# One hybrid layer on one core: no gather rows from the 364th to the dense loop, the low part of the U tile behind the slot's rows, inputs loaded earlier, the last norms interleaved

## The chip, the cores and the metric

The kernel runs on one core of a Trainium2 chip. The time is the device time of one execution in microseconds; lower is better. Engines are named as the profile names them: PE (TensorE) multiplies matrices, DVE (VectorE) and ACT (ScalarE) work elementwise, POOL (GpSimd) issues indirect DMAs (gathers), SP (SyncE) issues most other DMAs. An engine runs its instructions in the order in which they stand, and so does SP's queue of DMA issues.

## What is computed

The reference is one layer on x of shape (1, 1024, 1024) in float32: a mixer (a gated linear recurrence and a state-space group, both behind one projection), added to x, then a retrieval feed-forward ("PEER"), added too, and a final RMS norm. The change lies in the second half:

```python
def block(xb):                       # 128 tokens at a time
    q = (xb @ wq).reshape(TOK_BLOCK, PEER_HEADS, PEER_QDIM)
    s1, s2 = q[..., :PEER_HALF] @ k1.T, q[..., PEER_HALF:] @ k2.T
    ...                              # top 16 of each, then top 16 of their sums: e, g
    u_sel = u_tab[e]                 # 8 heads x 16 experts of 16384
    act = gelu(einsum('thkd,td->thk', u_sel, xb))
    return einsum('thk,thkd->td', g * act, v_tab[e])
...
h = h + peer_ffn(rms_norm(h, norm2_g), ...)
return rms_norm(h, normf_g)
```

Each of the 1024 tokens picks 128 of 16384 experts; each expert is a row of `u_tab` and a row of `v_tab`.

## The kernel before

The 1024 tokens are 8 blocks of 128. Three blocks (NG = 3) are computed as the formula stands: for each of the 128 experts per token a row of U is gathered for all 128 tokens (one indirect DMA of 512 KB on POOL, L1263) and multiplied with the token's x and summed by one DVE instruction (`CUSTOM_DVE_ANT_0 row<-row,xg` in the profile, `ISA row,act<-row,xg` in the order of instructions). After 128 such U rows, Gelu and the gates, 128 V rows are gathered and accumulated into `hb` (`SCALAR_TENSOR_TENSOR hb<-row,act,hb`). One of these 256 steps of a block is called a row here: 3 x 256 = 768 rows in all. `mg.units` counts them; the pool `rows` holds eight (ROWS = 8), so that at most seven gathers are asked ahead. `xg` (x of the block) and `hb` (the residual) come by DMA, and `finish` norms a block and stores it.

The other five blocks (ND = 5) are computed densely, against all 16384 experts: `first` multiplies a tile of U (128 experts) with all 640 tokens and applies Gelu, a gate matrix G weighs the result, and `second` multiplies it with V and accumulates over all experts. Floats are split in a high and a low part (`uh`, `ul`; `vh`, `vl`; `hh`, `hl`; the high part by ACT, the low part by DVE), and each product is three matmuls.

This runs in two stages.

- *The early stage.* `ahead` computes `first` for 97 of the 128 tiles and stores the results in DRAM (A_d, L1412), loading U tiles (`ur`, L1318). `build` makes the gate matrix: top-k on DVE, one-hot tiles (`ohA`, `ohB`), matmuls (`gp`), copies into `gs` by ACT, and stores of 2 MB of `gs` into G_d (L1218). The rows run beside this. The order is set by a planner (`Merge`): every piece of work is a generator, engines have planned busy times, and the generator with the lowest planned time plus a bias goes next. What a generator yields it waits for: None, the name of a flag, or a function. After a function has come true, the generator's time is put to PE's planned time. Rows have a pace of at least 2 us; `gate` yields None in this stage.
- *The dense loop.* 32 turns `c` of four tiles each, in an order written out by hand. In a turn PE does `first` for one tile of the next turn (48 matmuls), then `second` for token blocks 0, 1, then 2, 3 and 4 tile by tile. `pair()` gives the PSUM for a block, with two buffers; `add` adds it to h (`h<-h,vp` on DVE). Between these pieces stand seven slots, `rows_of(0)` to `rows_of(6)`; each lets so many rows run as bring the spent share of the rows that are left up to its part of a turn. Here rows ignore the gate. `raw` has three buffers for the U and V loads (`ur` L1505, `vr` L1352); loads stand where an earlier user has just freed one.

`prologue` leads from one stage to the other: the first V tiles, G tiles (`gt`, L1454) and A_d tiles (`hr`, L1348). The pools of V lie where `gs` lay. `last` is the end of the final turn: `second` for blocks 2, 3, 4, each followed by the `finish` of the block before, with its own load of the norm's weights `nf` (L1308) and its store (L1313).

Of the kernel before, what the change touches and what calls it, by code (L numbers as in the profile page):

```python
# [7 lines left out]
F32 = mybir.dt.float32  # L8
# [4 lines left out]
AF = mybir.ActivationFunctionType  # L13
# [5 lines left out]
P = 128  # L19
D = 1024  # L20
# [952 lines left out]
GT = 32  # L973
ROWS = 8
PACE = 2.0


def peer(tc, a, cst, pools, h, nx, mg):
# [25 lines left out]
    def split_to(hi, lo, src):  # L1004
        S.activation(hi, src, AF.Copy)
        V.tensor_tensor(lo, src, hi.bitcast(F32), ALU.subtract)
# [269 lines left out]
        return r  # L1276

    def gate():
        return (lambda: mg.units < share[0]) if share else None

    def gather(n):

        xg = gp.tile([P, D], F32, name="xg", tag="xg", bufs=1)
        nc.sync.dma_start(xg, X_d[n])
        act = gp.tile([P, P], F32, name="act", tag="act", bufs=1)
        for k in range(P):
            ub = take()
            yield gate()
            V.tensor_tensor_reduce(ub, ub, xg, 1.0, 0.0, ALU.mult, ALU.add, act[:, k:k + 1])
            mg.units += 1  # L1290
        hb = gp.tile([P, D], F32, name="hb", tag="hb", bufs=1)
        nc.sync.dma_start(hb, H_d[n])
        S.activation(act, act, AF.Gelu_apprx_tanh)
        yield
        V.tensor_tensor(act, act, gw[n], ALU.mult)
        yield
        for k in range(P):
            vb = take()
            yield gate()
            V.scalar_tensor_tensor(hb, vb, act[:, k:k + 1], hb, ALU.mult, ALU.add)  # L1300
            mg.units += 1
        finish(ND + n, hb)
        yield

    def finish(b, x):
        sq = rows.tile([P, D], F32, name="sqf", tag="row")
        nf = rows.tile([P, D], F32, name="nf", tag="row")
        nc.sync.dma_start(nf, a["gf"].partition_broadcast(P))  # L1308
        st = gp.tile([P, 3], F32, name="st", tag="st")
        S.activation(sq, x, AF.Square, accum_out=st[:, 0:1])  # L1310
        rsqrt_cols(mg, st[:, 1:2], st[:, 2:3], st[:, 0:1], 1.0 / D)
        V.scalar_tensor_tensor(x, x, st[:, 2:3], nf, ALU.mult, ALU.mult)
        nc.sync.dma_start(out_v[:, b], x)  # L1313
# [159 lines left out]
    def rows_of(slot):  # L1473

        spread[0] += SLOTS[slot] / sum(SLOTS) * left / (nch - 0.6)
        while mg.units < 2 * NG * P and left - (2 * NG * P - mg.units) + 1 <= spread[0]:
            row()

    def second(p_, b, t, first, last):
        bs = slice(b * P, b * P + P)  # L1480
        for i in range(2):
# [25 lines left out]
    def split_u(c):  # L1507
        uh = pu.tile([P, 8, P], F32R, tag="uh", name="uh")
        ul = pu.tile([P, 8, P], F32R, tag="ul", name="ul")
        split_to(uh, ul, raw_u.pop(c))  # L1510
        return uh, ul

    def prologue():
        now = [tile(0, n) for n in range(JC)]
# [49 lines left out]
    def dense():  # L1564
        now = [tile(0, n) for n in range(JC)]
        u = nextu.pop()
        carry = None
        for c in range(nch):
            more = c + 1 < nch
            nx = [tile(c + 1, n) for n in range(JC)]  # L1570

            now[3].high()
            fs = ()
            if more:
                nx[2].hr = phh.tile([P, TD], F32, name="ha", tag="ha", bufs=1)
# [12 lines left out]

            pr = [pair()]
            for jj, t in enumerate(now):  # L1590
                second(pr[0], 0, t, jj == 0, jj == JC - 1)
            if c + 2 < nch:
                u = split_u(c + 2)
            load_v(c + 1, 2)
            rows_of(1)

            if more:
                nx[0].turn()
            pr.append(pair())
            for jj, t in enumerate(now):  # L1600
                second(pr[1], 1, t, jj == 0, jj == JC - 1)
            add(0, pr[0])
            if not more:
                finish(0, acc[0])
            rows_of(2)
            if not more:
                last(now, pr)
                return

            pr.append(pair())  # L1610
            for jj, t in enumerate(now):
                second(pr[2], 2, t, jj == 0, jj == JC - 1)
                if jj == 0:
                    second(total, 4, t, c == 0, False)
                    add(1, pr[1])
                    nx[0].weigh()
                    rows_of(3)
                    pr.append(pair())
                second(pr[3], 3, t, jj == 0, jj == JC - 1)
                if jj:  # L1620
                    second(total, 4, t, False, False)
                if jj:
                    nx[jj].weigh()
                    nx[jj - 1].low_h()
                    if jj == 1:
                        load_h(c + 2, 0)
                    elif jj == 2:
                        load_h(c + 2, 1)
                    rows_of(3 + jj)
                    if jj == 3:  # L1630
                        weights(c + 2) if c + 2 < nch else None
                        add(2, pr[2])
                    nx[jj - 1].low_v()
                    if jj == 1:
                        load_v(c + 1, 3)
                    elif jj == 2:
                        load_u(c + 3)
                    else:
                        load_v(c + 2, 0)
                if jj < 3:  # L1640
                    nx[jj + 1].turn()
                    nx[jj].high()
            carry = 3, pr[3]
            now = nx

    def last(now, pr):

        for b in (2, 3, 4):
            p_ = pair() if b < 4 else total
            for jj, t in enumerate(now):  # L1650
                second(p_, b, t, b < 4 and jj == 0, jj == JC - 1)
            if b == 2:
                add(1, pr[1])
                finish(1, acc[1])
            else:
                add(b - 1, p0)
                finish(b - 1, acc[b - 1])
            p0 = p_
        add(4, total)
        finish(4, acc[4])  # L1660

    with tc.manual_schedule():
        dense()
# [81 lines left out]
```

## Time and profile before

| | us |
|---|---|
| median of 3 runs | 2668.85 (2663.75 to 2673.37) |
| profiled execution, its own time | 2657.8 |
| its span from first to last instruction | 2656.0 |
| PE busy | 2508.6 (94%) |
| DVE busy | 2363.7 (89%) |
| ACT busy | 1322.6 (50%) |
| POOL busy | 1157.8 (44%) |
| start of the first `second` matmul of the dense loop (chain of waits) | 1541.0 |

Times in the views are from the span's start. A row of a timeline has start, duration, engine, line, operation, output<-inputs and, in brackets, how long the engine was idle before it and what ended that. Most lines are L146, a helper that records every operation, so work is told apart by its tiles. SPq and POOLq are DMA issues; their duration is the time that the issue held the queue. A wait for several things is put down to the one that came last.

### The profile page before, as it was taken

Reading aid. Unit: us, or ns where it says so; the run is one execution under the profiler, and the core shown is the slowest. Engines: PE = TensorE matmul, PEld = TensorE weight load, DVE = VectorE, ACT = ScalarE, POOL = GpSimd, SP = SyncE. Lnnn points to the kernel's source line nnn. Section 1 sums busy time; section 2 is a strip of 40 time slices with the busy share of each in tenths; the row PEclk is TensorE's granted clock in tenths of the full one; section 3 lists DMA queues with packets and bytes.
Section 4 is the critical chain, followed back from the end, with each engine's and each line's share of the span. In section 5 each row is a group of like instructions: output and inputs, shape, how many; then the busy total and the mean of one; then the engine's idle time right before and its main releaser. Section 6 shows DMA issues by size and latency. Waiting matters only on the chain.

```text
span 2656.0 us, 40788 instructions
## 1 busy us (share of the span) xinstructions
PE 2508.6 (94%) x14623; PEld 2272.5 (86%) x14623; DVE 2363.7 (89%) x4549; ACT 1322.6 (50%) x2404; POOL 1157.8 (44%) x777
## 2 busy tenths in 40 slices
PE   7998999998999999999999699999899999999996
PEld 6776889998999999998999688888788888888885
DVE  7898559998999999999999589999888888999996
ACT  5566334332774956838749443344444343333333
POOL 0000000353754847748547345554445545555440
PEclk9999999999999999999999899999999999999998
DMA  5113124687999999999989989999899999999994
GB/s 176 34 44 108 59 88 136 227 280 273 326 382 317 366 378 309 393 330 365 398 277 388 373 316 333 328 330 329 306 327 323 329 326 327 329 329 331 331 325 131
DMA packets 302971, 755.40 MB, mean 284 GB/s; under 512 B 28976, under 2 KB 127472, under 8 KB 298032
## 3 DMA queue, kind: packets, MB, share of 16 engines
q0 software_dynamic: 110592, 402.70, 42.1%
q1 hardware_dynamic: 186480, 339.95, 36.1%
q10 hardware_dynamic: 5696, 10.15, 1.1%
q8 instruction: 115, 1.88, 0.3%
q14 instruction: 88, 0.72, 0.1%
HBM read 665.54 MB, written 85.98 MB: 283 GB/s over the span
## 4 chain that ended last, share of the span: by engine, by line
PE 59%; DVE 23%; DMA 9%; ACT 5%; issue 3%; SPq 0%; ACTq 0%; DVEq 0%
PE vp L146 25%; PE ap L146 16%; PE total L146 6%; DMA A_d<-aa 4%; PE qp L146 3%; PE gp L146 3%; ACT ohB L146 3%; PE wop L146 3%; DVE oh L146 2%; DVE row L146 2%; DVE ul L146 2%; DMA ur<-in_uT_dram 1%; DVE hb L146 1%; DVE ix L146 1%; DVE ci L146 1%
## 5 line engine op out<-in xcount | busy, mean ns | idle before, releaser
L1263 POOL DMA_INDIRECT row<-in_peer_u_dram,idx x384 | 560.9, 1461 | 942.9 <-DVE scv L146 473.7
L1263 POOL DMA_INDIRECT row<-in_peer_v_dram,idx x384 | 594.2, 1547 | 456.9 <-DVE hb L146 332.3
L146 PE MATMUL ap<-xDl,uh 128*128 128x320 f32 x2048 | 654.4, 320 | 26.0 <-ACT aa L146 25.3
L146 PE MATMUL ap<-xDh,ul 128*128 128x320 f32 x2048 | 646.9, 316 | 9.0 <-DVE ul L146 8.9
L146 PE MATMUL ap<-xDh,uh 128*128 128x320 f32 x2048 | 644.8, 315 | 0.0
L146 DVE SCALAR_TENSOR_TENSOR hb<-row,act,hb 128x1024 f32<-128x1024 f32 x384 | 491.7, 1280 | 4.4
L146 DVE CUSTOM_DVE_ANT_0 row<-row,xg 128x1024 f32<-128x1024 f32 x384 | 458.5, 1219 | 12.8 <-DMA xg<-X_d 7.3
L146 PEld LDWEIGHTS ap<-xDl,uh 128*128 128x128 f32 x2048 | 391.8, 191 | 30.1 <-ACT aa L146 27.8
L146 PE MATMUL vp<-vl,hh 128*128 128x512 f32 x1024 | 400.5, 391 | 11.6 <-DVE vl L146 9.8
L146 PEld LDWEIGHTS ap<-xDh,ul 128*128 128x128 f32 x2048 | 391.5, 191 | 12.1 <-DVE ul L146 10.7
L146 PE MATMUL vp<-vh,hl 128*128 128x512 f32 x1024 | 399.6, 390 | 0.0
L146 PE MATMUL vp<-vh,hh 128*128 128x512 f32 x1024 | 399.5, 390 | 0.0
L146 PEld LDWEIGHTS ap<-xDh,uh 128*128 128x128 f32 x2048 | 391.0, 191 | 0.0
L146 ACT ACTIVATE gq<-gt 128x640 f32<-128x640 f32 x128 | 175.3, 1369 | 328.8 <-DVE hr L146 324.4
L146 DVE TENSOR_TENSOR ul<-ur,uh 128x1024 fp32r<-128x1024 f32 x128 | 155.8, 1218 | 92.5 <-ACT uh L146 92.5
L146 PEld LDWEIGHTS vp<-vl,hh 128*128 128x128 f32 x1024 | 193.0, 188 | 52.4 <-DVE vl L146 10.7
L146 PEld LDWEIGHTS vp<-vh,hh 128*128 128x128 f32 x1024 | 192.9, 188 | 40.3
L146 PEld LDWEIGHTS vp<-vh,hl 128*128 128x128 f32 x1024 | 193.0, 189 | 38.8
L146 PE MATMUL gp<-ohB,ohA 128*128 128x128 f32 x1280 | 198.1, 281 | 24.5 <-ACT gs L146 16.9
L146 ACT ACTIVATE aa<-ap 128x320 f32<-128x320 f32 x194 | 84.8, 438 | 244.0 <-PE ap L146 194.7
L146 ACT ACTIVATE ohB<-ohB,kt 128x128 f32<-128x128 f32 x480 | 205.1, 502 | 0.0
L146 PEld LDWEIGHTS gp<-ohB,ohA 128*128 128x128 f32 x1280 | 179.4, 193 | 30.0 <-ACT gs L146 18.0
(442 smaller groups left out, 4488.3 us busy)
## 6 DMA issues: line engine op xcount, KB each, us to landing
ur<-in_uT_dram SPq DMA_DIRECT2D x128, 512.0 KB, 6.5
vr<-in_peer_v_dram SPq DMA_DIRECT2D x128, 512.0 KB, 6.2
gt<-G_d SPq DMA_DIRECT2D x32, 1280.0 KB, 9.4
G_d<-gs SPq DMA_DIRECT2D x19, 2048.0 KB, 25.6
A_d<-aa SPq DMA_DIRECT2D x96, 320.0 KB, 8.6
hr<-A_d SPq DMA_DIRECT2D x96, 320.0 KB, 5.8
wqr<-in_wq_dram SPq DMA_DIRECT2D x31, 512.0 KB, 3.9
row<-in_peer_u_dram,idx POOLq DMA_INDIRECT x384, 7.4
```

Of the source, the lines that this page charges most:

```text
L146: return fn(*args, **kw)
L1263: G.indirect_dma_start(out=r, out_offset=None, in_=a["peer_v" if at >= P else "peer_u"], in_offset=bass.IndirectOffsetOnAxis(ap=idx[n][:, ...
```

## The change

Four edits, in the order of the diff.

1. `gate` now yields a function in the early stage too: a row goes on while fewer than EARLY = 363 are done. So from the 364th on no row runs until the dense loop, which takes all that are left. As the gate is a function, every early row also has its planned time put to PE's.
2. `xg` of the next block is loaded right after the last U row of a block instead of at the next block's start, and `hb` after the 65th U row instead of after the last.
3. `split_u` is cut in two: ACT's `uh` stays where it was, DVE's `ul` comes behind `rows_of(1)`.
4. `last` loads `nf` once, and the norms of blocks 0 to 4 are generators whose steps stand between the matmul groups; block 4 is finished in two halves of 512 columns.

```diff
+EARLY = 363
...
     def gate():
-        return (lambda: mg.units < share[0]) if share else None
+        return lambda: mg.units < (share[0] if share else EARLY)
+
+    held = []
+    def fetch_xg(n):
         xg = gp.tile([P, D], F32, name="xg", tag="xg", bufs=1)
         nc.sync.dma_start(xg, X_d[n])
+        return xg
+
+    def gather(n):
+        xg = fetch_xg(n) if n == 0 else held.pop()
         act = gp.tile([P, P], F32, name="act", tag="act", bufs=1)
         for k in range(P):
             ub = take()
             yield gate()
             V.tensor_tensor_reduce(ub, ub, xg, 1.0, 0.0, ALU.mult, ALU.add, act[:, k:k + 1])
             mg.units += 1
-        hb = gp.tile([P, D], F32, name="hb", tag="hb", bufs=1)
-        nc.sync.dma_start(hb, H_d[n])
+            if k == P // 2:
+                hb = gp.tile([P, D], F32, name="hb", tag="hb", bufs=1)
+                nc.sync.dma_start(hb, H_d[n])
+        if n + 1 < NG:
+            held.append(fetch_xg(n + 1))
...
     def split_u(c):
         uh = pu.tile([P, 8, P], F32R, tag="uh", name="uh")
         ul = pu.tile([P, 8, P], F32R, tag="ul", name="ul")
-        split_to(uh, ul, raw_u.pop(c))
-        return uh, ul
+        r = raw_u.pop(c)
+        S.activation(uh, r, AF.Copy)
+        yield
+        V.tensor_tensor(ul, r, uh.bitcast(F32), ALU.subtract)
+        yield uh, ul
...
-            if c + 2 < nch:
-                u = split_u(c + 2)
+            su = split_u(c + 2) if c + 2 < nch else None
+            if su:
+                next(su)
             load_v(c + 1, 2)
             rows_of(1)
+            if su:
+                u = next(su)
...
     def last(now, pr):
+        nf = rows.tile([P, D], F32, name="nf", tag="row")
+        nc.sync.dma_start(nf, a["gf"].partition_broadcast(P))
+
+        def norm(b):
...
+            if b < 4:
+                S.activation(sq, x, AF.Square, accum_out=st[:, 2:3])
+                yield
+            else:
+                for i in range(2):
+                    xi = x[:, 512 * i:512 * i + 512]
+                    V.tensor_tensor(xi, xi, total[:, i], ALU.add)
+                    V.tensor_tensor_reduce(sq[:, 512 * i:512 * i + 512], xi, xi, 1.0, 0.0, ALU.mult, ALU.add,
+                                           st[:, i:i + 1])
+                    yield
+                V.tensor_tensor(st[:, 2:3], st[:, 0:1], st[:, 1:2], ALU.add)
...
+        for jj, t in enumerate(now):
+            second(total, 4, t, False, jj == JC - 1, (0,))
+        add(3, p0)
+        next(g[3])
+        for _ in g[2]:
+            pass
+        for jj, t in enumerate(now):
+            second(total, 4, t, False, jj == JC - 1, (1,))
```

How this moves instructions shows at three places. The first is DVE at the end of the early stage. Before, up to the first weighing of an A_d tile (`ul` belongs to U tiles of `ahead`, `vl` to V tiles of `prologue`; of the nine V rows that run in this stage the last four are shown):

```order
L146 TENSOR_TENSOR ul_16172<-ur_16169,uh_16171 128x1024
L146 SCALAR_TENSOR_TENSOR hb_16176<-row_16140,act_12642,hb_16176 128x1024
L146 SCALAR_TENSOR_TENSOR hb_16176<-row_16213,act_12642,hb_16176 128x1024
L146 SCALAR_TENSOR_TENSOR hb_16176<-row_16216,act_12642,hb_16176 128x1024
L146 SCALAR_TENSOR_TENSOR hb_16176<-row_16252,act_12642,hb_16176 128x1024
L146 TENSOR_TENSOR vl_16182<-vr_16107,vh_16180 128x1024
L146 TENSOR_TENSOR vl_16256<-vr_16210,vh_16254 128x1024
L146 TENSOR_TENSOR hr_16284<-hr_16284,gq_16292 128x640
```

Now, the same place:

```order
L146 TENSOR_TENSOR ohA_15988<-iota_63,kt_14751 128x512
L146 TENSOR_SCALAR ohB_15989<-iota_63,kt_14751 128x128
L146 TENSOR_TENSOR ul_16028<-ur_16025,uh_16027 128x1024
L146 TENSOR_TENSOR ul_16114<-ur_16111,uh_16113 128x1024
L146 TENSOR_TENSOR vl_16119<-vr_16055,vh_16117 128x1024
L146 TENSOR_TENSOR vl_16152<-vr_16147,vh_16150 128x1024
L146 TENSOR_TENSOR hr_16187<-hr_16187,gq_16192 128x640
```

393 rows stood ahead of the dense loop before and 363 do now; the order of the other work there is the same but for small exchanges.

The second place is DVE in a turn of the dense loop, from the last `vl` of the turn's tiles to the add of block 1 (h1). Before:

```order
L146 TENSOR_TENSOR vl_22699<-vr_22585,vh_22659 128x1024
L146 TENSOR_TENSOR ul_22755<-ur_22621,uh_22754 128x1024
L146 SCALAR_TENSOR_TENSOR hb_22252<-row_22521,act_19293,hb_22252 128x1024
L146 SCALAR_TENSOR_TENSOR hb_22252<-row_22539,act_19293,hb_22252 128x1024
L146 SCALAR_TENSOR_TENSOR hb_22252<-row_22542,act_19293,hb_22252 128x1024
L146 SCALAR_TENSOR_TENSOR hb_22252<-row_22581,act_19293,hb_22252 128x1024
L146 TENSOR_TENSOR h0_2450<-h0_2450,vp_22729 128x1024
L146 SCALAR_TENSOR_TENSOR hb_22252<-row_22617,act_19293,hb_22252 128x1024
L146 SCALAR_TENSOR_TENSOR hb_22252<-row_22694,act_19293,hb_22252 128x1024
L146 TENSOR_TENSOR h1_2451<-h1_2451,vp_22774 128x1024
```

Now:

```order
L146 TENSOR_TENSOR vl_18941<-vr_18824,vh_18901 128x1024
L146 SCALAR_TENSOR_TENSOR hb_14717<-row_18778,act_12834,hb_14717 128x1024
L146 SCALAR_TENSOR_TENSOR hb_14717<-row_18781,act_12834,hb_14717 128x1024
L146 SCALAR_TENSOR_TENSOR hb_14717<-row_18820,act_12834,hb_14717 128x1024
L146 TENSOR_TENSOR ul_18997<-ur_18860,uh_18996 128x1024
L146 TENSOR_TENSOR h0_2450<-h0_2450,vp_18971 128x1024
L146 SCALAR_TENSOR_TENSOR hb_14717<-row_18856,act_12834,hb_14717 128x1024
L146 SCALAR_TENSOR_TENSOR hb_14717<-row_18890,act_12834,hb_14717 128x1024
L146 SCALAR_TENSOR_TENSOR hb_14717<-row_18936,act_12834,hb_14717 128x1024
L146 TENSOR_TENSOR h1_2451<-h1_2451,vp_19013 128x1024
```

`ul` has moved behind the three or four rows of its slot, and a turn has 13 rows (12 in a few) where it had 12 (11 in a few). The norm of the second gathered block stands, in its turn, between the adds of h0 and h1 now, and stood ahead of the add of h2 before.

The third place is SP at the very end. Before, and so on to block 4:

```order
L1308 DMA nf_25224<-in_gf_dram 128x1024
L1313 DMA out_0_dram<-hb_22252 128x1024
L1308 DMA nf_25264<-in_gf_dram 128x1024
L1313 DMA out_0_dram<-h0_2450 128x1024
L1308 DMA nf_25304<-in_gf_dram 128x1024
L1313 DMA out_0_dram<-h1_2451 128x1024
L1308 DMA nf_25344<-in_gf_dram 128x1024
```

Now:

```order
L1318 DMA nf_25224<-in_gf_dram 128x1024
L1323 DMA out_0_dram<-hb_21060 128x1024
L1663 DMA nf_25263<-in_gf_dram 128x1024
L1694 DMA out_0_dram<-h0_2450 128x1024
L1694 DMA out_0_dram<-h1_2451 128x1024
L1694 DMA out_0_dram<-h2_2452 128x1024
```

One load of `nf` serves all five blocks; the two half stores of block 4 and the store of block 3 follow.

More of the change, by code (lines that the diff above doesn't have):

```diff
@@ L1278, in gate @@
     def gate():
-        return (lambda: mg.units < share[0]) if share else None
-    def gather(n):
+        return lambda: mg.units < (share[0] if share else EARLY)
+    held = []
+    def fetch_xg(n):
         xg = gp.tile([P, D], F32, name="xg", tag="xg", bufs=1)
         nc.sync.dma_start(xg, X_d[n])
+        return xg
+    def gather(n):
+        xg = fetch_xg(n) if n == 0 else held.pop()
         act = gp.tile([P, P], F32, name="act", tag="act", bufs=1)
@@ L1477, in rows_of, with second @@
             row()
-    def second(p_, b, t, first, last):
+    def second(p_, b, t, first, last, halves=(0, 1)):
         bs = slice(b * P, b * P + P)
-        for i in range(2):
+        for i in halves:
             ns = slice(512 * i, 512 * i + 512)
@@ L1603, in dense @@
             if not more:
-                finish(0, acc[0])
-            rows_of(2)
-            if not more:
                 last(now, pr)
                 return
+            rows_of(2)
             pr.append(pair())
@@ L1646, in last @@
     def last(now, pr):
-        for b in (2, 3, 4):
-            p_ = pair() if b < 4 else total
-            for jj, t in enumerate(now):
[L1651 to L1657, printed above, removed]
-            p0 = p_
-        add(4, total)
-        finish(4, acc[4])
+        nf = rows.tile([P, D], F32, name="nf", tag="row")
@@ new lines, in last @@
+        nc.sync.dma_start(nf, a["gf"].partition_broadcast(P))
+        def norm(b):
+            st = gp.tile([P, 5], F32, name="st4", tag="st4", bufs=2)
+            sq = rows.tile([P, D], F32, name="sqf", tag="row")
+            x = acc[b]
+            if b < 4:
[9 more added lines that the diff above has]
+                V.tensor_tensor(st[:, 2:3], st[:, 0:1], st[:, 1:2], ALU.add)
+            v, dst = st[:, 3:4], st[:, 4:5]
+            V.tensor_scalar(v, st[:, 2:3], 1.0 / D, EPS, ALU.mult, ALU.add)
+            S.activation(dst, v, AF.Sqrt)
+            yield
+            V.reciprocal(dst, dst)
+            V.tensor_tensor(v, v, dst, ALU.mult)
+            V.tensor_tensor(v, v, dst, ALU.mult)
+            V.tensor_scalar(v, v, -0.5, 1.5, ALU.mult, ALU.add)
+            V.tensor_tensor(dst, dst, v, ALU.mult)
+            yield
+            n = 1 if b < 4 else 2
+            for i in range(n):
+                ns = slice(D // n * i, D // n * (i + 1))
+                V.scalar_tensor_tensor(x[:, ns], x[:, ns], dst, nf[:, ns], ALU.mult, ALU.mult)
+                nc.sync.dma_start(out_v[:, b, ns], x[:, ns])
@@ new lines, in last @@
+        g = [norm(b) for b in range(5)]
+        next(g[0])
+        rows_of(2)
+        p0 = pr[1]
+        for b in (2, 3):
+            p_ = pair()
+            for jj, t in enumerate(now):
+                second(p_, b, t, jj == 0, jj == JC - 1)
+            add(b - 1, p0)
+            next(g[b - 1])
+            for _ in g[b - 2]:
+                pass
+            p0 = p_
+        for jj, t in enumerate(now):
+            second(total, 4, t, False, jj == JC - 1, (0,))
+        add(3, p0)
@@ L1662, in peer @@
+        next(g[3])
+        for _ in g[2]:
+            pass
+        for jj, t in enumerate(now):
+            second(total, 4, t, False, jj == JC - 1, (1,))
+        next(g[4])
+        next(g[3])
+        next(g[4])
+        next(g[4])
+        next(g[3])
+        next(g[4])
+        for n in (4, 3):
+            for _ in g[n]:
+                pass
     with tc.manual_schedule():
```

## The prediction

> **What bounds the kernel now.** I read first the page's busy shares, then the span in stretches, then the waits and the timelines of the stretches that stand out. The shares leave two candidates, TensorE and VectorE:
>
> ```profile
> PE 2508.6 (94%) x14623; PEld 2272.5 (86%) x14623; DVE 2363.7 (89%) x4549; ACT 1322.6 (50%) x2404; POOL 1157.8 (44%) x777
> ```
>
> The stretches (us, then busy time of PE, PEld, DVE, ACT, POOL with counts, granted TensorE clock, DMA share, GB/s) separate them. Three turns of the dense loop, then four pieces around its start:
>
> ```profile
> 1842.00:1876.25 34.25, 34.25 (x169) 29.58 (x168) 30.37 (x29) 14.81 (x17) 13.80 (x11) 1.00 0.92 327
> 1876.25:1919.75 43.50, 35.88 (x170) 30.48 (x169) 33.68 (x50) 16.60 (x20) 19.68 (x14) 0.92 0.82 292
> 1919.75:1954.00 34.25, 34.25 (x170) 29.57 (x169) 30.38 (x42) 13.76 (x15) 16.42 (x13) 1.00 0.92 330
> ...
> 1461.17:1469.88 8.71, 0.00 (x1) 0.00 (x0) 0.51 (x1) 1.59 (x3) 0.80 (x1) 0.69 1.03 420
> 1469.88:1506.38 36.50, 36.04 (x240) 35.48 (x240) 32.03 (x44) 21.44 (x54) 23.85 (x19) 0.93 1.04 382
> 1506.38:1519.32 12.94, 0.00 (x1) 0.00 (x1) 1.29 (x2) 2.33 (x3) 0.00 (x0) 0.60 1.05 357
> 1519.32:1541.00 21.68, 20.04 (x121) 19.42 (x122) 14.30 (x15) 13.65 (x17) 1.86 (x1) 0.92 0.89 322
> ```
>
> A dense turn is PE without a gap: 34.25 of 34.25 us, with DVE idle for 34.25 - 30.37 = 3.9 us. One turn is 43.50 us long, 9.25 more than its neighbours. Just before the dense loop PE stands still twice, 8.71 and 12.94 us, while DVE and ACT stand still too and the DMA share is over 1: this entry is bound by transfers. The chain of waits gives the turn's two parts on PE, 48 matmuls of `first` and 12 of `second`:
>
> ```profile
> 1560.05 2.72 PE vp L146 x12
> ...
> 1568.21 7.04 PE ap L146 x48
> ```
>
> 7.04 + 5 blocks x 24 x 0.227 = 34.2 us, as measured.
>
> **Term 1, the entry: no rows from the 364th.** The 363rd row on DVE, then DVE's groups of row work from 1439.4 to 1504 us, and the page's row on the gathers' landing:
>
> ```profile
> 1438.13 1.21 DVE L146 CUSTOM_DVE_ANT_0 row<-row,xg 128x1024 f32<-128x1024 f32 x1
> ...
> L146 DVE CUSTOM_DVE_ANT_0 row<-row,xg 128x1024 f32<-128x1024 f32 x21 | 25.0, 1222 | 0.0
> L146 DVE SCALAR_TENSOR_TENSOR hb<-row,act,hb 128x1024 f32<-128x1024 f32 x9 | 11.6, 1285 | 0.3
> ...
> row<-in_peer_u_dram,idx POOLq DMA_INDIRECT x384, 7.4
> ```
>
> So 21 + 9 = 30 rows leave this stretch: before, 393 were done by the dense loop, now 363. With each goes a gather of 512 KB on POOL's queue. What PE's two stops hang on, in the timelines of ACT and SP:
>
> ```profile
> 1437.46 17.90 SPq L1412 DMA_DIRECT2D A_d<-aa  x1
> 1468.29 1.06 ACT L146 ACTIVATE uh<-ur 128x1024 fp32r<-128x1024 f32 x1 [10.49 <-DMA ur<-in_uT_dram]
> 1492.95 0.81 SPq L1218 DMA_DIRECT2D G_d<-gs  x2
> 1499.06 14.62 SPq L1454 DMA_DIRECT2D gt<-G_d  x1
> 1516.94 2.00 ACT L146 ACTIVATE vh<-vr 128x1024 fp32r<-128x1024 f32 x2 [17.13 <-DMA G_d<-gs]
> 1519.70 0.38 SPq L1318 DMA_DIRECT2D ur<-in_uT_dram  x1
> ```
>
> The first stop is a late `ur` load: SP was held 17.9 us on an A_d store behind a G_d store. The second is `vh`, which takes over the memory of `gs` and waits until the last G_d store has read it. Both go back to a G_d store of 2 MB that drains slowly. DMA packets by queue, first 1500 to 1510 us, then 1470 to 1475 us:
>
> ```profile
> q0 software_dynamic: 976, 3.55, 87.0%
> q1 hardware_dynamic: 1003, 0.51, 17.0%
> ...
> q1 hardware_dynamic: 2785, 1.55, 99.7%
> ```
>
> Beside the gathers (q0) the store gets 1003 packets in 10 us, one for one with the gathers' 976; nearly alone it gets 2785 in 5 us, 5.6 times as fast. Its 4096 packets (2 MB in 512 B pieces) then take 4096 / 557 = 7.4 us instead of the 24 us from 1492.95 to 1516.94. Row 363 is done at 1439.3 us and the 7 gathers asked ahead land some 8 us later (7.4 in the row above), so from about 1447 us the stores run nearly alone. The first stop then vanishes: ACT reaches `uh` at about 1458 us in either case, and the load has landed. That is 8.7 us, and 2 of the clock after it (0.93 over 36.5 us is 2.6 us lost): 11. The last G_d store ends some 11 us after the last `gs` instead of 24, which takes the second stop away at its old place. But what stands behind it on SP stays a chain: `gt`, two A_d stores, then `ur` (1519.70), then `uh` and `ul`, 7.2 us from that issue to the end of `ul` by the timeline; PE has one group of 24 matmuls (3.5 us) to cover it. I leave 4 us of a stop there: 12.9 - 4 = 9, and 2 us each for the clock and for two short stops between 1519 and 1527: 13. **Term 1: -24 us**, bounds -28 (21.65 us of stops, 4.3 us of clock, the short stops) and -11 (only the first stop goes). The ACT and PE orders there are the old ones, so nothing else moves.
>
> The gate is also asked for every row before that, which shifts early rows by up to 6 places against the U tiles. The stage up to there:
>
> ```profile
> 680.00:1438.00 758.00, 724.55 (x5076) 715.83 (x5075) 735.53 (x1759) 525.35 (x1291) 478.14 (x302) 0.98 0.97 353
> ```
>
> PE is busy for 96% of it, so an order can win or lose little; I take 0, bounds +4 and -4, about a tenth of the 33 us that PE is idle there.
>
> **Term 2, the inputs early.** DVE, then PE, in the long turn:
>
> ```profile
> 1873.90 1.28 DVE L146 SCALAR_TENSOR_TENSOR hb<-row,act,hb 128x1024 f32<-128x1024 f32 x1
> ...
> 1880.09 1.21 DVE L146 TENSOR_TENSOR h<-h,vp 128x1024 f32<-128x1024 f32 x1
> ...
> 1891.60 1.22 DVE L146 CUSTOM_DVE_ANT_0 row<-row,xg 128x1024 f32<-128x1024 f32 x1 [7.29 <-DMA xg<-X_d]
> ...
> 1895.17 0.79 PE L146 MATMUL vp<-vl,hh 128*128 128x512 f32 x1 [7.62 <-DVE vl L146]
> 1895.76 0.63 PE L146 MATMUL vp<-vh,hl 128*128 128x512 f32 x1
> ```
>
> The row waits for `xg`, `vl` is queued behind it on DVE, and PE waits 7.62 us for `vl`, then runs slowly (0.63 for 0.39). With `xg` fetched 128 rows ahead all of it goes: -9.25 us. But the row block's norm in that turn stays: from the end of the last row (1873.90 + 1.28) to 1880.09 it costs DVE 4.9 us, and now it lies in another place, between the adds of h0 and h1. `pair()` has two buffers, so block 3 cannot start before h1 is added: PE asks for it 7.04 + 2 x 5.44 + 2.72 = 20.6 us into the turn. From DVE's part of a turn:
>
> ```profile
> 2510.60 1.23 DVE L146 TENSOR_TENSOR ul<-ur,uh 128x1024 fp32r<-128x1024 f32 x1 [1.96 <-ACT uh L146]
> ...
> 2515.58 1.21 DVE L146 TENSOR_TENSOR h<-h,vp 128x1024 f32<-128x1024 f32 x1
> 2516.71 3.96 DVE L146 SCALAR_TENSOR_TENSOR hb<-row,act,hb 128x1024 f32<-128x1024 f32 x3
> 2520.59 1.21 DVE L146 TENSOR_TENSOR h<-h,vp 128x1024 f32<-128x1024 f32 x1
> ```
>
> This turn began on PE at 1919.75 + 17 x 34.25 = 2502.0, so h1 is added from 18.6 to 19.8 us, 0.8 before it is asked for. With 4.9 us more and some tenths won by `ul`, it ends at about 24: PE stops for 3.5 us. Stops of that size are followed by slow matmuls; the nearest row is the last turn, where a wait of 2.2 us is followed by this:
>
> ```profile
> 2611.43:2614.90 3.47, 3.47 (x8) 2.79 (x9) 3.40 (x3) 0.00 (x0) 0.00 (x0) 0.51 0.00 0
> ```
>
> 3.47 us at half clock, 1.7 lost. So +5, bounds 0 (the norm is absorbed as it is now) and +8. **Term 2: -9.2 + 5 = -4 us.** The Trainium skill (TensorE: Matmul & The Clock Gate, Part 1) says that the clock halves after an idle window of about 3.4 us. The row above shows half clock after a wait of only 2.2 us, so the trace does not bear the threshold out; by the page the stop might cost no clock, and the sum would be 1.7 us lower.
>
> **Term 3, 30 rows more in the dense loop, and `ul` behind them.** 405 rows over 31.4 turns are 12.9 a turn instead of 11.9: 1 x 1.285 us more DVE work, against 3.9 us of idle time. Of that idle time 1.96 in the turn shown is `ul` waiting for ACT's `uh`. Now rows run in that time and `ul` follows at about 12 us into the turn, when `uh` is long there. PE wants `ul` at the next turn's start, 22 us later. What is queued behind the moved `ul`: on DVE the add of h0, which waits for PE's block 0 (12.5 us) anyway; on SP the `vr` load of the third tile, which takes the raw buffer that `ul` frees, now some 4 us later; its tile's turn on ACT comes with PE's third tile group, 7.04 + 2 x 5.44 + 2 x 4.08 = 26 us into the turn, 13 us after that. **Term 3: 0**, hidden by PE's 34.25; if nothing hid it, 30 x 1.285 = +39 us.
>
> **Term 4, the end.** The six norms each load `nf` again. The tile's waits, PE's last matmul, and the last block's DVE and SP rows:
>
> ```profile
>   DMA nf<-in_gf_dram: 6.4, 5
> ...
> 2638.39 0.39 PE L146 MATMUL total<-vh,hh 128*128 128x512 f32 x1
> 2645.37 1.21 DVE L146 TENSOR_TENSOR h<-h,total 128x1024 f32<-128x1024 f32 x1
> 2650.44 1.28 DVE L146 SCALAR_TENSOR_TENSOR h<-h,st,nf 128x1024 f32<-128x1024 f32 x1 [1.24 <-DMA nf<-in_gf_dram]
> 2651.75 0.34 SPq L1313 DMA_DIRECT2D out_dram<-h  x1
> ```
>
> PE is done at 2638.8 but the last add starts at 2645.4, since each norm waits for its own `nf`. With one `nf` the adds follow PE. After PE's last matmul (I put it 0.8 later: one more row stands ahead of the last `vl`) there remain a half add and a half square (0.65 each), two chains of small operations (1 each), two half scalings (0.65) and one whole (1.28), so that the last DVE operation ends at about 2646.4 instead of 2651.7. The 4.3 us behind it (span 2656.0) stay. **Term 4: -5 us**, bounds -3 and -7.
>
> **Sum.** -24 - 4 + 0 - 5 = -33 us. The profiled execution took 2657.8 us (span 2656.0), so 2625 for one like it. It is 11 us under the median of the runs, 2668.85; the terms do not depend on what makes that difference, so I set the forecast at 2668.85 - 33 = **2636 us**.
>
> **Rivals.**
> 1. *The entry is only half relieved.* The second stop stays, because `gt`, the A_d stores and the loads behind the last G_d store take over its length. For it: `gt` alone is 1280 KB, and A_d, `hr`, `vr` and `ur` all follow it on SP, with the DMA share still 0.89 after 1519 us with no gathers. Against it: PE only needs the `ur` of them. Then 11 instead of 24: -20, 2649 us.
> 2. *DVE becomes the bound in the dense loop.* The idle time that `ul` left is lost again at the adds, which wait for PE, and the added row lies on the path: +1.2 x 31 = 37 us, 2668.85 - 33 + 37 = 2673 us, no change. Against it: idle time that is a wait for PE is slack by definition; for it: h1's add has only 0.8 us.
> 3. *The late `vr` load makes it slower.* It decides once the load takes over 13 us from its issue: then ACT's `vh` of the third tile is late in every turn. Each 1.5 us of delay costs 31 x 1.5 = 46 us: 2668.85 - 33 + 46 = 2682 us. For it: the DMA share of 0.92 rises by a gather a turn. Against it: 327 GB/s is far from the 420 of the entry.
> 4. *More than the sum:* both stops go entirely and the finishing norm stops nobody, -28 - 9 - 5 = -42, 2627 us.
>
> That the rows are not held back at all is excluded by the order of the built kernel: no row stands between the 363rd and the dense loop.
>
> **How the numbers follow.** Forecast 0.64, with a range of its own of 2626 to 2646; rival 1 0.18, rival 4 0.07, rival 2 0.06, rival 3 0.05. The range of 2618 to 2656 takes in rivals 1 and 4 and leaves out 2 and 3; both ends have some us for the spread of the runs, which is 10. A measurement of this kernel tells 0.3% (8 us) from no change: faster 0.64 + 0.18 + 0.07 = 0.89, same 0.06, slower 0.05.
>
> **What would show it.** Right: no PE stop over 6 us between 1438 us and the first `vp`, which starts at about 1517 instead of 1541; SP's issues behind the last G_d store under 10 us; all dense turns 34.25 us but one of about 39; one `nf` load in the end, the last DVE operation within 8 us of the last matmul. Wrong: a `vh` that still waits over 10 us for G_d, dense turns over 34.5 us with PE waiting for `vl` or h, or a row that waits for its gather.

## The result, and the profile after

Beside runs of the kernel before, the changed kernel took 2622.3 us (median of 4, 2619.9 to 2627.2) against 2666.9: a ratio of 0.985 (0.981 to 0.988), faster by 44.6 us. Its profiled execution took 2620.7 us with a span of 2619.0, against 2657.8 and 2656.0: 37.0 us less. The forecast of 2636 us was 14 us too high: inside the stated range of 2618 to 2656, but below the 2626 to 2646 that the forecast itself was given.

First the busy line of the page after the change, then the span in stretches: the two longest stops of PE before the dense loop, the long turn, an ordinary turn, and the end from the start of the last full turn (columns as in the prediction: busy PE, PEld, DVE, ACT, POOL, granted clock, DMA share, GB/s).

```profile
PE 2503.9 (96%) x14623; PEld 2268.0 (87%) x14623; DVE 2365.3 (90%) x4556; ACT 1321.8 (50%) x2402; POOL 1130.8 (43%) x777
...
1451.98:1453.57 1.59, 0.00 (x0) 0.00 (x0) 0.50 (x1) 1.59 (x3) 0.00 (x0) 1.00 1.04 418
1492.24:1494.55 2.31, 0.00 (x0) 0.00 (x0) 0.25 (x1) 1.54 (x3) 0.00 (x0) 1.00 1.03 344
1882.01:1922.13 40.12, 36.20 (x169) 30.63 (x168) 34.38 (x43) 16.41 (x19) 18.02 (x13) 0.96 0.88 319
1922.13:1956.44 34.31, 34.31 (x169) 29.57 (x168) 30.86 (x43) 15.16 (x16) 18.20 (x13) 1.00 0.92 327
2539.69:2619.00 79.31, 62.31 (x289) 51.73 (x287) 62.47 (x92) 22.40 (x33) 14.47 (x11) 0.94 0.48 172
```

The stops of 8.71 and 12.94 us have become 1.59 and 2.31. The same end took 85.60 us before:

```profile
2570.40:2656.00 85.60, 64.40 (x289) 52.78 (x287) 59.90 (x85) 23.89 (x35) 11.51 (x10) 0.90 0.51 176
```

The timelines of SP and ACT show why the stops went: what stands behind a G_d store on SP, and what waits for it on ACT.

```profile
1427.72 18.17 SPq L1422 DMA_DIRECT2D A_d<-aa  x1
1448.94 0.86 SPq L1219 DMA_DIRECT2D G_d<-gs  x1
1449.90 9.16 SPq L1422 DMA_DIRECT2D A_d<-aa  x1
1475.29 0.80 SPq L1219 DMA_DIRECT2D G_d<-gs  x2
1476.86 4.40 SPq L1464 DMA_DIRECT2D gt<-G_d  x1
...
1451.98 1.06 ACT L146 ACTIVATE uh<-ur 128x1024 fp32r<-128x1024 f32 x1 [3.68 <-DMA ur<-in_uT_dram]
1485.03 2.01 ACT L146 ACTIVATE vh<-vr 128x1024 fp32r<-128x1024 f32 x2 [2.88 <-DMA G_d<-gs]
```

While the last gathers run (to some 1447 us) the issue behind a G_d store still holds SP for 18.17 us; without gathers the next one holds it for 9.16, and `gt` behind the last store for 4.40 instead of 14.62. `vh` waits 2.88 us for G_d instead of 17.13, `uh` 3.68 instead of 10.49. From the issue of the last G_d store to the start of that `vh` it is 9.7 us (1475.29 to 1485.03), and 24.0 before.

Row 363 and the first `second` matmul, on DVE and PE:

```profile
1435.71 1.22 DVE L146 CUSTOM_DVE_ANT_0 row<-row,xg 128x1024 f32<-128x1024 f32 x1
...
1511.74 0.39 PE L146 MATMUL vp<-vl,hh 128*128 128x512 f32 x1
```

Between the two lie 76.0 us, and 102.7 before (1438.13 to 1540.84); this stretch is called the entry below. The 37.0 us of the two profiles are therefore: 2.4 ahead of row 363, 26.7 in the entry, 1.6 in the dense loop (the long turn 3.4 shorter, 28 others 0.06 longer each), 6.3 at the end.

What is left of the long turn, on DVE and then on PE, is the norm of the second gathered block between the adds of h0 and h1:

```profile
1899.72 0.15 DVE L146 TENSOR_SCALAR st<-st 128x1 f32<-128x1 f32 x1 [1.22 <-ACT sqf L146]
1901.24 0.16 DVE L146 RECIPROCAL st<-st 128x1 f32<-128x1 f32 x1 [1.36 <-ACT st L146]
1903.19 1.28 DVE L146 SCALAR_TENSOR_TENSOR hb<-hb,st,nf 128x1024 f32<-128x1024 f32 x1 [1.02 <-DMA nf<-in_gf_dram]
1905.54 1.21 DVE L146 TENSOR_TENSOR h<-h,vp 128x1024 f32<-128x1024 f32 x1
...
1906.81 0.57 PE L146 MATMUL vp<-vl,hh 128*128 128x512 f32 x1 [3.92 <-DVE h L146]
```

The chain reads from the bottom: PE waits 3.92 us for h1's add, which stands behind a norm in which DVE itself waits three times, 3.6 us in all. This profile shows the turn at its shortest: in five others whose dense loop has the same order (below: the changed kernel again, the hold without the planner's function, the two that bring back half of a row, and the shifted tiles) it took 42.0 to 42.4 us.

### The profile page after: what moved, and what is told of

The parts are those of the page before. It is cut to its first block, busy times and chain, and to the rows that moved or that the text cites. A ratio compares the mean times of both kernels' runs of the same rounds, so it can differ in the third digit from the quotient of the medians.

```text
span 2619.0 us, 40771 instructions
## 1 busy us (share of the span) xinstructions
PE 2503.9 (96%) x14623; PEld 2268.0 (87%) x14623; DVE 2365.3 (90%) x4556; ACT 1321.8 (50%) x2402; POOL 1130.8 (43%) x777
## 4 chain that ended last, share of the span: by engine, by line
PE 62%; DVE 22%; DMA 7%; ACT 4%; issue 3%; ACTq 0%; SPq 0%; DVEq 0%
PE vp L146 26%; PE ap L146 17%; PE total L146 7%; PE qp L146 4%; DMA A_d<-aa 3%; PE gp L146 3%; PE wop L146 3%; DVE row L146 2%; DVE oh L146 2%; DVE ul L146 2%; DVE hb L146 2%; ACT ohB L146 1%; DVE ix L146 1%; DVE ci L146 1%; DVE v L146 1%
## 5 line engine op out<-in xcount | busy, mean ns | idle before, releaser
L1264 POOL DMA_INDIRECT row<-in_peer_v_dram,idx x384 | 563.2, 1467 | 440.6 <-DVE hb L146 302.4
L146 PE MATMUL gp<-ohB,ohA 128*128 128x128 f32 x1280 | 183.7, 278 | 17.9 <-ACT gs L146 8.9
L146 DVE TENSOR_TENSOR h<-h,vp 128x1024 f32<-128x1024 f32 x128 | 155.7, 1217 | 48.8 <-PE vp L146 48.5
L146 PEld LDWEIGHTS gp<-ohB,ohA 128*128 128x128 f32 x1280 | 169.7, 192 | 22.2 <-ACT gs L146 9.7
```

Of the source, the lines that this page charges most:

```text
L146: return fn(*args, **kw)
L1264: G.indirect_dma_start(out=r, out_offset=None, in_=a["peer_v" if at >= P else "peer_u"], in_offset=bass.IndirectOffsetOnAxis(ap=idx[n][:, ...
```

## Experiments

### Each edit alone

The four edits were put into the kernel before one by one, as they stand in the diff.

Edit 1 alone (`EARLY` and `gate`):

> The kernel before with the first edit alone (363 rows ahead of the dense loop, every early row gated by a function). Theory of the terms as the change's trace shows them: the first vp starts 29 us earlier than before (1541 to about 1512), the long turn of 43.5 us and the end stay as they were, and the added row per turn is hidden: 29 us faster, ratio 0.989. Rival, the first edit needs the third: with ul still in front of the slot's rows, DVE's idle time of 3.9 us a turn cannot take the added row of 1.3 us in full, turns grow to 34.6 us or more, and 10 us or more of the 29 go back: ratio 0.993 or above.

Measured: ratio 0.990 (0.987 to 0.992), 28 us. From row 363 to the first `vp` it is 76.3 us (1444.0 to 1520.3), as in the changed kernel. The rival's mechanism is there too, but smaller than the 10 us that it asked for: eight turns are 35.0 us long. Here are the turn before them and the first two, and PE in the first:

```profile
1581.80:1616.03 34.23, 34.23 (x169) 29.57 (x168) 31.89 (x31) 13.88 (x15) 18.13 (x13) 1.00 0.92 332
1616.03:1651.02 34.99, 34.54 (x169) 29.49 (x168) 32.11 (x31) 13.71 (x15) 18.12 (x13) 1.00 0.92 330
1651.02:1686.02 35.00, 34.56 (x169) 29.49 (x168) 32.49 (x32) 13.65 (x15) 17.16 (x13) 1.00 0.93 342
...
1637.30 0.50 PE L146 MATMUL vp<-vl,hh 128*128 128x512 f32 x1 [0.45 <-DVE h L146]
```

DVE is idle for over 2 us of such a turn (in the first, `ul` waits 2.39 us for `uh`), and still PE waits for h1's add: the idle time lies ahead of the rows, where it covers nothing. 8 x 0.74 = 6 us, and a long turn of 46.0 instead of 43.5. In the changed kernel, with `ul` behind the rows, no ordinary turn has a gap. That this is edit 3's doing is read from the order; edits 1 and 3 were not run without the others.

Edit 2 alone (`xg` and `hb` early):

> The kernel before with the second edit alone (xg after the last U row, hb after the 65th). Theory: the wait of 7.3 us for xg goes and the finishing norm stays where it was, ahead of the add of h2, where it is absorbed: the long turn of 43.5 us becomes 34.3, 9 us faster, ratio 0.9965, nothing else moves. Rival: the norm costs its turn wherever it stands (5.8 us in the changed kernel) and was covered by the wait for xg: the long turn becomes 39 to 40 us, 3.5 us faster, ratio 0.9987.

Measured: ratio 0.996 (0.994 to 0.998), 10 us. The turn of 43.5 us is 35.54, with PE at 34.89. DVE there:

```profile
1890.04:1925.58 35.54, 34.89 (x170) 29.41 (x169) 33.41 (x50) 16.49 (x19) 20.22 (x14) 1.00 0.91 336
...
1892.64 1.29 DVE L146 SCALAR_TENSOR_TENSOR hb<-hb,st,nf 128x1024 f32<-128x1024 f32 x1
1893.84 1.22 DVE L146 TENSOR_TENSOR h<-h,vp 128x1024 f32<-128x1024 f32 x1
1894.97 1.22 DVE L146 TENSOR_TENSOR vl<-vr,vh 128x1024 fp32r<-128x1024 f32 x1
```

At its old place the same norm costs 1.3 us. So of the 5.8 us of the changed kernel (8.0 in its second profile) all but 1.3 are the price of the place to which the norm has moved, not of the norm.

Edit 3 alone (`ul` behind the rows):

> The kernel before with the third edit alone (ul behind the rows of its slot), 12 rows a turn as before. Theory: PE bounds every turn, so turns stay 34.25 us and the time is the same (ratio 1.000 within 0.002); DVE's idle time per turn stays 3.9 us in sum, but moves from ul to the adds. Rival: the later ul frees its raw buffer later and the third V tile's load comes late: turns grow by 0.5 us or more, ratio 1.006 or above. If turns come out at 34.31 as in the changed kernel, the 0.06 us belong to this edit and not to the added rows.

Measured: ratio 1.000 (0.998 to 1.001), as the theory has it. All ordinary turns are 34.25 us.

Edit 4 alone (the end):

> The kernel before with the fourth edit alone (one load of nf, interleaved norms, halved block 4). Theory: the end gets 6 us shorter as in the changed kernel (85.6 to 79.3 us from the start of the last full turn to the end of the span), ratio 0.9977. Rival: part of the 6 us came from the earlier edits (12 or 13 rows in the last turns at other places), and this edit alone gives 4 us or less, ratio 0.9985 or above.

Measured: ratio 0.998 (0.997 to 1.000), 5.5 us. Here is its end, and a turn of its dense loop, which has 12 rows as before:

```profile
2577.70:2659.50 81.80, 65.27 (x289) 53.68 (x287) 61.29 (x91) 22.41 (x33) 11.43 (x10) 0.91 0.43 155
...
1744.90:1779.22 34.32, 34.32 (x169) 29.58 (x169) 31.12 (x30) 13.82 (x15) 18.89 (x12) 1.00 0.91 331
```

The end is 3.8 us shorter in this profile, 6.3 in the changed kernel's; the section on the hardware finds the difference. And the 0.06 us by which every turn of the changed kernel is longer belong to this edit, though it touches nothing in the loop.

The four medians give 28 + 10 + 0 + 5.5 = 44 us together, as much as the whole change. That they fit so well is in part luck: in the profiles edit 1 alone loses 6 us in eight turns that the changed kernel does not lose, and edit 2 alone gains 8.0 us in the long turn (43.50 to 35.54) where the changed kernel gains 3.4 or less.

### What the entry waited for: the gathers or the rows' work

Both kernels start from the changed one. In the first, operations of a row's size come back without gathers:

```diff
+                for _ in range(30):
+                    if share:
+                        break
+                    mg.at(mg.cur["p"])
+                    mg.cur["p"] = mg.cur["t"] + pace[0]
+                    yield
+                    V.tensor_tensor_reduce(old, xg, xg, 1.0, 0.0, ALU.mult, ALU.add, act[:, k:k + 1])
```

> The changed kernel, with some 24 DVE operations of a row's size put back behind row 363 at a row's pace (x times x into a used row buffer), without their gathers. Theory, the entry was bound by the gathers' traffic: it stays at 76 to 80 us from row 363 to the first vp, no PE stop over 5 us, the store of G_d holds SP as short as in the changed kernel, and the time stays within 4 us of it (ratio 0.985 to 0.986). Rival, the entry was bound by DVE's row work: the entry grows by 20 us or more and the ratio is 0.992 or above.

Measured: ratio 0.984 (0.981 to 0.987), that of the changed kernel. DVE's added work in the entry, and SP behind the last two G_d stores:

```profile
L146 DVE CUSTOM_DVE_ANT_0 row<-xg 128x1024 f32<-128x1024 f32 x24 | 29.3, 1222 | 0.5
...
1460.13 9.30 SPq L1432 DMA_DIRECT2D A_d<-aa  x1
1487.84 4.13 SPq L1474 DMA_DIRECT2D gt<-G_d  x1
```

29.3 us of row work came back, and the entry is 73.5 us long (1448.67 to 1522.19), with no stop of PE over 1.8 us. DVE's work was not what it waited for.

In the second, gathers come back, each behind an operation on one column in place of a row's work:

```diff
+                again = [[ub, 0.0]] + [list(asked[EARLY + i]) for i in range(1, ROWS - 1)]
+                for i in range(30):
+                    r = again[i % (ROWS - 1)]
...
+                    V.tensor_copy(r[0][:, 0:1], mg.lastA[:, 0, 0:1])
...
+                    G.indirect_dma_start(out=r[0], out_offset=None, in_=a["peer_u"],
```

> The changed kernel, with 24 gathers put back behind row 363 at a row's pace (the rows already asked for are fetched again into the same buffers), each behind a DVE operation on one column instead of a row's work. Theory, the gathers slow the stores of G_d: PE's two stops come back (some 9 and 13 us), the issue behind the last G_d store is held 14 us again, the time from row 363 to the first vp is 95 us or more instead of 76, and the ratio is 0.992 to 0.994. Rival, DVE's row work bound the entry: it stays at 76 to 80 us and the ratio at 0.985.

Measured: ratio 0.992 (0.990 to 0.995). Two stops of PE of 7 us are back; SP and ACT:

```profile
1501.97:1508.90 6.93, 0.00 (x1) 0.00 (x1) 0.18 (x3) 0.49 (x2) 3.79 (x5) 0.61 1.03 419
1521.90:1528.97 7.07, 0.00 (x0) 0.00 (x0) 1.28 (x2) 2.33 (x3) 0.00 (x0) 0.65 1.04 297
...
1472.55 0.70 SPq L1219 DMA_DIRECT2D G_d<-gs  x1
1473.34 18.33 SPq L1441 DMA_DIRECT2D A_d<-aa  x1
...
1508.41 0.44 ACT L146 ACTIVATE aa<-ap 128x320 f32<-128x320 f32 x1 [13.89 <-DMA A_d<-aa]
1515.52 1.06 ACT L146 ACTIVATE uh<-ur 128x1024 fp32r<-128x1024 f32 x1 [5.86 <-DMA ur<-in_uT_dram]
1526.60 2.00 ACT L146 ACTIVATE vh<-vr 128x1024 fp32r<-128x1024 f32 x2 [9.69 <-DMA G_d<-gs]
```

The issue behind a G_d store holds SP for 18.33 us again. PE's first stop hangs on that hold by another last link than before the change: ACT's `aa` waits 13.89 us for an A_d store, of those that stand behind the hold, where before it was `uh` that waited for its late load (here it does so later, for 5.86 us). The second stop is the old one, `vh` behind G_d. In size it is about half, and less than the 95 us expected: the entry is 89.5 us (1461.4 to 1550.9), 13 above the changed kernel's 76, where the 30 gathers of before made 26. There are 23 gathers here, the first issued at 1470.0 us, 9 after row 363, and the last at 1510.9; whether the missing half hangs on that or on the gathers and the work together was not tried.

### The hold without the planner's function

```diff
-        return lambda: mg.units < (share[0] if share else EARLY)
+        return None if not share and mg.units < EARLY else lambda: bool(share) and mg.units < share[0]
```

> The changed kernel, but the gate yields None for rows below 363, as before, and holds from there: the hold without the planner's function. Theory: the function moves nothing that counts; the start of row 363 lies anywhere between 1435 and 1451 us, which is what kernels with one early order show already, the time from row 363 to the first vp is 76 us as in the changed kernel (103 before), and the ratio to before is that of the changed kernel, 0.9846 within 0.003. Rival: the function saves 8 us ahead of row 363 (1446 against 1436), and the ratio here is 0.9876.

Measured: ratio 0.988 (0.985 to 0.992), which is the rival's figure; the theory's 0.9846 lies at the edge of the interval. Row 363 starts at 1448.4 us, and the entry is 78.8, as the theory has it. And the changed kernel itself once more, on another chip:

> The changed kernel itself again, beside the next three on one chip. Expected: ratio 0.9846 within 0.003, turns of 34.31 us, the long turn at 40.1. Open is the start of row 363 (1435.7 in its first profile): if it lies at another place of 1435 to 1461 us here, with the same instructions, the 8 us that the first profile gained ahead of the entry are spread between executions and no effect of the planner's function; if it is at 1436 again, the function has moved it.

Measured: ratio 0.983 (0.980 to 0.985). Row 363 starts here at 1441.3 us instead of 1435.7, the entry is 78.0 us. What lies ahead of row 363 varies between executions and kernels by more than the 4 us put as the function's bound, while the entry does not:

| kernel | row 363 | first vp | entry |
|---|---|---|---|
| before | 1438.1 | 1540.8 | 102.7 |
| edit 2 alone | 1451.0 | 1554.6 | 103.5 |
| edit 3 alone | 1450.3 | 1550.4 | 100.2 |
| edit 4 alone | 1443.0 | 1546.2 | 103.2 |
| changed | 1435.7 | 1511.7 | 76.0 |
| changed, again | 1441.3 | 1519.3 | 78.0 |
| edit 1 alone | 1444.0 | 1520.3 | 76.3 |
| hold, no function | 1448.4 | 1527.2 | 78.8 |

So the hold gives 25 us (mean of the first four less mean of the last four: 102.4 - 77.3 = 25.1). Whether the function gives some us ahead of row 363 stays open. The medians lean that way: without it the kernel is 29.6 us under the one before, with it 44.6 and 45.6. The profiles do not: row 363 starts at 1444.6 us on the mean of seven with the function (1431.2 to 1461.4) and at 1446.2 on the mean of five without it (1438.1 to 1451.0).

### Room for one more row

```diff
-EARLY = 363
+EARLY = 333
```

> The changed kernel with EARLY = 333, so that 435 rows instead of 405 lie in the dense loop, 14 a turn instead of 13. DVE is idle for 1.6 to 3.2 us of a turn now, a row takes 1.2 to 1.3. Theory, there is room for one row a turn and no more, and the entry has nothing more to give: turns stay at 34.3 us but for a few, the time from the last gp to the first vp stays at 37 us, and the time is that of the changed kernel within 6 us (ratio 0.982 to 0.987). Rival: DVE becomes the bound, PE waits for vl in most turns, turns of 35 us, 20 us or more slower than the changed kernel (0.992 or above).

Measured: ratio 0.980 (0.977 to 0.983), a little under the range expected; the interval reaches into that of the changed kernel, whose first profile is only 1.1 us longer. The dense loop is as the theory has it. Turns with 13 and 14 rows, and the one with the norm:

```profile
1709.10:1743.40 34.30, 34.30 (x169) 29.57 (x168) 33.68 (x33) 13.76 (x15) 17.92 (x14) 1.00 0.97 362
1743.40:1777.70 34.30, 34.30 (x169) 29.57 (x168) 33.14 (x31) 13.84 (x15) 18.50 (x14) 1.00 0.94 344
1949.30:1986.99 37.69, 34.97 (x170) 29.35 (x169) 37.40 (x51) 15.43 (x17) 22.85 (x15) 1.00 0.92 340
```

DVE is down to some 0.6 us of idle time in such turns, and PE still has no gap. The first `vp` starts at 1510.3 us, as in the changed kernel: holding the rows back 30 earlier finds nothing more to relieve.

### The norm spread over rows, and the place of the tiles

```diff
-        finish(ND + n, hb)
+        if share and n + 1 < NG:
+            fin.append(steps(ND + n, hb))
+        else:
+            finish(ND + n, hb)
...
             mg.units += 1
+            step()
```

`steps` is `finish` cut in four: square, square root, Newton step, scaling with the store; `step` runs one of them behind a row.

> The changed kernel, with the norm of the second gathered block cut into four steps that stand one, two and five rows apart behind the first rows of the next block. Theory, the long turn is DVE waiting inside the norm (1.2, 1.4 and 1.0 us) between the adds of h0 and h1: with the waits covered by rows the turn becomes 34.3 to 35.5 us instead of 40.1, 5 us faster than the changed kernel (0.998 of it). Rival: the turn is long because of the norm's own 1.8 us of DVE work and the load of nf; it stays at 38 us or above.

Measured: 2612.8 us beside 2621.3 for the changed kernel on that chip, ratios 0.982 (0.979 to 0.984) and 0.983 (0.980 to 0.985): the medians differ by 8.5 us, the intervals overlap. The profile is clear: the turn with the norm, and DVE in it.

```profile
1877.00:1911.30 34.30, 34.30 (x170) 29.56 (x169) 32.34 (x41) 16.40 (x19) 16.47 (x12) 1.00 0.92 338
...
1895.17 1.22 DVE L146 TENSOR_TENSOR h<-h,vp 128x1024 f32<-128x1024 f32 x1 [0.43 <-PE vp L146]
1898.19 0.15 DVE L146 TENSOR_SCALAR st<-st 128x1 f32<-128x1 f32 x1
1899.40 0.15 DVE L146 RECIPROCAL st<-st 128x1 f32<-128x1 f32 x1
```

No wait stands behind the norm's operations any more, and the turn is as long as the others; in the changed kernel's second profile it was 42.3.

```diff
-            st = gp.tile([P, 5], F32, name="st4", tag="st4", bufs=2)
+            st = gp.tile([P, 16], F32, name="st4", tag="st4", bufs=2)
```

> The changed kernel, with the small tile of the end norms (five columns, two buffers) widened to 16 columns, so that the tiles of hh, hl, vh, vl, uh and ul lie 64 bytes lower: at the same place modulo 128 bytes as before the change. Turns were 34.31 us in all kernels with the fourth edit and 34.25 in all without it. Theory, the place of the tiles in SBUF makes the 0.06 us: turns become 34.25, 1.8 us in all. Rival: the place has nothing to do with it, turns stay at 34.31.

Measured: ratio 0.986 (0.984 to 0.989). One turn:

```profile
1553.00:1587.27 34.27, 34.27 (x170) 29.58 (x169) 31.71 (x41) 14.07 (x17) 20.17 (x13) 1.00 0.97 358
```

All ordinary turns are 34.27 us, with the order of every engine unchanged. The place of the tiles makes two thirds of the 0.06; the rest is open, and so is what it is about the place that counts. It is worth 1 us in all and is lost in the time ahead of row 363 (1449.7 us here).

> The changed kernel with both, and EARLY = 333. Theory: what the runs with each showed adds up: turns of 34.25 us with 14 rows, no turn over 35.5 us, first vp where EARLY = 333 had it beside its own row ahead; 8 to 12 us under the changed kernel (0.995 to 0.997 of it, 0.980 of before). Rival: with 14 rows a turn DVE has no room for the norm's steps (0.6 us idle in some turns), the turn with the norm stays at 37 us or above and little of it comes.

Measured: 2623.7 us, ratio 0.984 (0.981 to 0.987), no better than the changed kernel. Within the dense loop it does what was expected, 34.27 us in every turn and none longer than 34.3; but its first `vp` starts at 1526.7 us, and the end has a stop of 4.1 us. The 8 to 12 us did not come: against the changed kernel's second profile the dense loop is 9.2 us shorter, the first `vp` 7.4 us later and the end 2.8 us longer.

## Why the prediction was right, and where its sizes were off

**Term 1, the entry, -24.** Right in mechanism and near in size: 26.7 between row 363 and the first `vp` of the two profiles, 25 over eight. The first stop was to vanish and left 1.59 us, since `uh` still waits for a `ur` that stood behind the hold of 18.17 us, while the last gathers ran. The last G_d store was to take some 11 us instead of 24, and it is 9.7. For the second I left 4 us, and it has 2.31, and 1.03 after it. "Issues behind the last G_d store under 10 us": 4.40 for `gt`. That it is the gathers is shown by the two kernels that brought back one half of a row each: row work alone gives no stop over 1.8 us, gathers alone give two of 7 us, which is about half of the effect; for the other half no run shows the cause. Rival 1 (`gt` and A_d take over the stop) is refuted by the length of that stop.

**The gate's shift of early rows, 0 with bounds of 4.** Not settled. The profiles differ by 2.4 us there, but kernels with nearly one order of early work differ by over 10, more than the bounds.

**Term 2, the inputs early, -9.2 + 5 = -4.** Measured -3.4 (43.50 to 40.12), with a stop of PE of 3.92 where 3.5 was worked out. That it comes so close is luck: in the second profile of the same program the turn is 42.31, with a stop of 4.82, and four other kernels with this loop have 42.0 to 42.4. So the norm costs 6 to 8 us there, up to the upper bound of 8 instead of the 5, and the term is mostly about -1. The place was read right from the order of instructions; that the old place costs only 1.3 us is what the kernel with this edit alone adds.

**Term 3, 30 rows more, 0.** Right, and so is the way: the rows run in the time in which `ul` used to wait. The 3.9 us of idle time that the term sets against the added row would not do by themselves: the kernel with edit 1 alone has the same room and loses 6 us, since what counts is the idle time between the rows and h1's add. The 0.06 us a turn (1.7 in all) are not the rows': edit 4 moved the tiles.

**Term 4, the end, -5.** Measured -6.3 and -3.8. The last DVE operation ends 7.6 us after the last matmul, as was said (within 8). The pieces that the term lists come to 5.9 us, though, and not to the 6.8 that its 2646.4 us needs behind a last matmul at 2639.6; the work took longer than the pieces, and PE, counted from the start of the last full turn, was done 0.6 us earlier (67.8 instead of 68.4) and not 0.8 later. What I did not see is that one and the same stop costs 0 or 3 us of clock.

**The sum, -33.** The profiles differ by 37.0, the medians by 44.6. The 4 us between 33 and 37.0 are 2.7 more in the entry, 1.3 more at the end and 2.4 ahead of row 363, less 2.4 in the dense loop, where 4 were forecast and 1.6 came. Of the rest of the 14 us, 1.9 are that the kernel before took 2666.9 beside this one and not 2668.85, and 7.6 lie between profiles and medians: the kernel before was profiled 9.1 us under its median, the changed one 1.6. In three kernels with nearly the same early work row 363 starts 5 to 13 us later than in that profile, so it is likely, but not shown, that the 7.6 us lie ahead of row 363. The step that failed is the sentence that the terms do not depend on what makes the difference between profile and median: one profile could not tell whether the change would move that too.

**Rivals 2 and 3** are refuted by the turns: PE has no gap but in the long one, and ACT waits for no `vr` load in the dense loop. What rival 2 describes, a late add of h1, is what the kernel with edit 1 alone shows.

**Rival 4** has the nearer time, 2627 us, but not the mechanism: the norm does stop PE, for 3.92 us or more, and the two stops of the entry are shorter and not gone. What the medians have beyond the profiles made its number come near.

## What to carry to other kernels

Bulk gathers on one queue can make a store of small packets on another queue much slower (here 24.0 us beside them, 9.7 without), and the stop then shows up at a third place, where something waits for the store's buffer or stands behind it in an issue queue; hold the gathers back there, not the arithmetic. An engine's idle time in a loop is room only if it lies between the added work and the operation that the bound engine waits for. When a wait is removed, look at what it had covered: here the norm behind it cost 1.3 us at one place and 6 to 8 at another, and spread over four rows nothing.

## What the hardware showed that was not expected

**The clock changes on a fixed grid.** In every profile the stretches of half clock are 3.41 us long or a whole multiple of it, but for the last, which the end cuts. The changed kernel and the one without the planner's function both have a PE stop of 2.8 us near the end. Three windows of the grid in each, the first kernel's first:

```profile
2586.35:2589.76 3.41, 1.63 (x8) 1.01 (x6) 2.23 (x7) 0.97 (x2) 0.00 (x0) 1.00 0.00 0
2589.76:2593.18 3.42, 2.38 (x10) 1.97 (x11) 2.27 (x3) 2.37 (x5) 0.00 (x0) 1.00 0.77 271
2593.18:2596.59 3.41, 3.41 (x16) 2.82 (x16) 2.08 (x6) 0.00 (x0) 0.00 (x0) 1.00 0.15 53
```

```profile
2604.24:2607.65 3.41, 1.31 (x6) 0.75 (x4) 2.55 (x7) 0.64 (x2) 0.00 (x0) 1.00 0.00 0
2607.65:2611.07 3.42, 2.71 (x6) 2.15 (x7) 2.23 (x5) 2.37 (x5) 0.00 (x0) 0.50 0.84 303
2611.07:2614.48 3.41, 3.41 (x9) 2.64 (x8) 1.79 (x5) 0.00 (x0) 0.00 (x0) 0.50 0.16 65
```

PE was busy for 1.63 of 3.41 us in the worst window of the first, and the clock stayed; for 1.31 in the second, and the next two windows ran at half. So the stop's position in the grid decides, and PE busy for 0.38 of a window (1.31 of 3.41) is little enough. The two do not give a sharp limit: in the entry of the changed kernel PE was busy for 1.92 us of the window from 1494.09 to 1497.50, and the next one ran at half clock too. The position makes the difference between an end of 79.3 us and one of 82.1, with the same instructions. The Trainium skill (TensorE: Matmul & The Clock Gate, Part 1) states a window of about 3.4 us that runs free of the kernel. The trace agrees with that: the window is 3.41 us, and in the two profiles of the changed kernel the grid lies 0.64 us apart. The prediction took that window for a limit on the length of a stop; as the rows here show, a stop need not fill a window to halve the clock.

**A turn of the dense loop depends on where its tiles lie.** With the same order on all engines, a shift of hh, hl, vh, vl, uh and ul, and of the tiles between them, by 64 bytes changed it from 34.31 to 34.27 us.

**The stage ahead of row 363 is not the same from one execution to the next.** Row 363 started between 1431 and 1461 us in the profiles, and 5.6 us apart in two of one and the same program. A change of a few us elsewhere is read from its own stage.
